# Gate and up products of a feed-forward step in seven block products

## The chip, the core and the metric

The kernel runs on one core of one Trainium2 chip. The metric is the device time of one execution in microseconds. Engines are named as in the profile: PE is TensorE's matmul side and PEld its weight loads, DVE is VectorE, ACT is ScalarE, POOL is GpSimd, SP is SyncE, which here only issues transfers. Each engine works through its own list of instructions in order and waits on semaphores for the others.

## The reference, cut to what matters

Two layers of a decoder trunk run over a prompt of 512 tokens and 8 x 4 sample tokens, 544 tokens in all, with a width of 1024. Four feed-forward half steps of this form stand before and behind the two mixers:

```python
def swiglu(x, w_gu, w_down):
    gate, up = jnp.split(x @ w_gu, 2, axis=-1)
    return (jax.nn.silu(gate) * up) @ w_down

def macaron_half(h, g, w_gu, w_down):
    return h + 0.5 * swiglu(rms_norm(h, g), w_gu, w_down)
```

`w_gu` has 1024 rows and 2 x 2816 columns, `w_down` 2816 rows and 1024 columns, all float32. The order of the stages is f10 (feed-forward 1 of layer 0), the even mixer, f20, f11, the odd mixer, f21.

## The kernel before, in words

Features lie on the partitions, tokens along the free axis: the residual is eight tiles `x` of 128 x 544. Every matrix product of weights (`mm`, L199) is made in three passes: weight and activation are each split into a high part in the float32r format and the rest, a low part (`wh`, `wl` for weights, `h`, `l` for activations), and high x high, high x low and low x high are summed in PSUM. One matmul has 128 x 128 weights and 272 tokens, so each k-tile of a 544-token product takes six matmuls, two halves `a` in the two banks of an `acc` tile. There are two `acc` tiles (two banks each) and four one-bank tiles `ps`.

A feed-forward step (`ffn`) has 22 inner rows `f` of 128 features. `hid(f)` makes one of them: the gate product (eight k-tiles, 48 matmuls), times `rbc`, the 1/rms of each token (L373), Silu on ACT (L374), times `rbc` again (L375), the up product (48 matmuls), the product of both (L378), and the split of the result into `h` and `l` (`split`, L209 on ACT and L210 on DVE). The weights of two inner rows come in one transfer each for gate and up (`stage`, L162, 256 columns, 1 MB) into one of two buffers `S`; `unit` cuts 128 columns out of it, ACT writes `wh` (L184) and DVE `wl` (L185). Each of `wh` and `wl` has two buffers, in a pool `wp` that lives through the whole program.

The inner rows are worked in three parts, (0, 7), (7, 15) and (15, 22). Behind the rows of a part, and one row of the next, its share of the down product is added to the eight `x` tiles (L395). Behind the last part `after_x` splits each finished `x` tile, times the next norm's gain, into the high and low parts (L212, L213) that the next stage multiplies, and adds its squares to `ssum`.

The order of instructions on each engine is set ahead of time by a scheduler that moves ready work forward by priority; weight parts have high priority. The mixers use `mm` too, and between them attention, a state space scan and other work that is not changed here. `mid` is a call in f10 that prepares the attention's position bias; it writes 3 MB from POOL's queue.

## Time and profile before

| what | value |
| --- | --- |
| time, median of 3 runs | 2400.13 us (2396.95 to 2403.28) |
| profiled execution: span | 2398.6 us |
| PE busy | 2367.8 us (99%), 18348 matmuls |
| DVE busy | 1182.6 us (49%) |
| ACT busy | 777.0 us (32%) |
| POOL busy | 163.8 us (7%) |
| read from and written to HBM | 203.69 MB and 17.75 MB |

The profiled execution gives its span from the first to the last instruction; it lies 1.5 us under the median of the runs, and no other time of this execution is shown. In the profile's groups, `acc<-h,wh` is a tile written from tiles read, with the buffer numbers left out. Matmuls overlap, so the mean time of one (about 290 ns) is not the pace at which they follow each other: that is a window's length divided by the count of matmuls in it. In a row of the windows view stand, for each engine, the busy time and the count of instructions, then the clock that was granted to TensorE, the busy share of the transfer engines, and GB/s. In a row of the timeline stand start, duration, engine, line, instruction, and in brackets the idle time before it with what ended it. Rows of one line show the count, the least, the middle and the greatest duration in ns.

### The profile page before, as it was taken

The numbers are of one execution on the slowest core, as the hardware profiler recorded it, in microseconds if no ns is written. First come the engines' busy times: TensorE is split into PE (matmuls) and PEld (weight loads), VectorE is DVE, ScalarE is ACT, GpSimd is POOL, SyncE is SP. The second block draws the span as 40 slices with busy tenths as digits, with TensorE's granted clock in tenths as the row PEclk, the third lists the DMA queues.
The fourth block names the chain that finished last, engine by engine and source line by source line (L and its number), as shares of the span: only waits on it lengthen the run. The fifth ranks groups of instructions, "written<-read, shape, count | busy, mean of one in ns | idle before, by whom it ended". The sixth has DMA issues, their size and how long they took to land.

```text
span 2398.6 us, 41806 instructions
## 1 busy us (share of the span) xinstructions
PE 2367.8 (99%) x18348; PEld 2296.9 (96%) x18348; DVE 1182.6 (49%) x1838; ACT 777.0 (32%) x1201; POOL 163.8 (7%) x199
## 2 busy tenths in 40 slices
...
GB/s 156 84 101 72 136 95 87 114 69 85 119 82 99 145 97 102 84 89 89 88 81 96 86 83 106 71 102 121 77 71 113 79 57 89 82 86 103 74 96 75
DMA packets 216677, 224.14 MB, mean 93 GB/s; under 512 B 8824, under 2 KB 208848, under 8 KB 216496
## 3 DMA queue, kind: packets, MB, share of 16 engines
q1 hardware_dynamic: 210312, 203.84, 26.4%
...
q8 instruction: 145, 2.38, 0.4%
...
HBM read 203.69 MB, written 17.75 MB: 92 GB/s over the span
## 4 chain that ended last, share of the span: by engine, by line
PE 76%; issue 19%; DVE 2%; DMA 2%; ACT 1%; POOL 1%; SPq 0%; POOLq 0%; ACTq 0%; DVEq 0%
PE acc L199 69%; DMA S<-in_ffn_w_down_dram 1%; PE ps L900 1%; PE ps L1129 1%; PE ps L609 1%; PE ps L1173 1%; PE ps L1168 1%; PE ps L601 0%; DMA S<-in_ffn_w_gu_dram 0%; PE ps L269 0%; PE ps L896 0%; PE ps L762 0%; PE ps L1056 0%; PE ps L620 0%; ACT sc L1146 0%
## 5 line engine op out<-in xcount | busy, mean ns | idle before, releaser
L199 PE MATMUL acc<-h,wh 128*128 128x272 f32 x5632 | 1178.6, 290 | 9.7 <-ACT wh L184 8.3
L199 PE MATMUL acc<-l,wh 128*128 128x272 f32 x5632 | 1179.8, 290 | 0.0
L199 PE MATMUL acc<-h,wl 128*128 128x272 f32 x5632 | 1174.4, 289 | 0.0
L199 PEld LDWEIGHTS acc<-h,wh 128*128 128x128 f32 x5632 | 888.5, 189 | 21.0 <-issue 9.1
L199 PEld LDWEIGHTS acc<-l,wh 128*128 128x128 f32 x5632 | 888.2, 189 | 11.1 <-issue 9.7
L199 PEld LDWEIGHTS acc<-h,wl 128*128 128x128 f32 x5632 | 888.4, 189 | 6.1 <-issue 5.2
L184 ACT ACTIVATE wh<-S 128x1024 fp32r<-128x1024 f32 (+1 forms) x361 | 375.2, 1040 | 1375.7 <-PE acc L199 1231.7
L185 DVE TENSOR_TENSOR wl<-S,wh 128x1024 fp32r<-128x1024 f32 (+1 forms) x361 | 436.9, 1210 | 64.9 <-ACT wh L184 54.9
L395 DVE SCALAR_TENSOR_TENSOR x<-acc,x 128x544 f32<-128x544 f32 x96 | 69.5, 724 | 285.4 <-PE acc L199 285.4
L378 DVE TENSOR_TENSOR hf<-acc,t 128x544 f32<-128x544 f32 x88 | 63.8, 725 | 275.6 <-PE acc L199 275.4
L373 DVE TENSOR_TENSOR t<-acc,rbc 128x544 f32<-128x544 f32 x87 | 63.1, 725 | 269.3 <-PE acc L199 269.1
L375 DVE TENSOR_TENSOR t<-t,rbc 128x544 f32<-128x544 f32 x88 | 63.3, 719 | 3.0 <-ACT t L374 3.0
L210 DVE TENSOR_TENSOR l<-hf,h 128x544 fp32r<-128x544 f32 x88 | 63.3, 719 | 2.2 <-ACT h L209 2.2
L209 ACT ACTIVATE h<-hf 128x544 fp32r<-128x544 f32 x88 | 57.3, 651 | 4.4 <-DVE hf L378 4.4
L374 ACT ACTIVATE t<-t 128x544 f32<-128x544 f32 x88 | 57.5, 653 | 2.1 <-DVE t L373 1.9
L256 POOL DMA_DIRECT2D xd<-x x16 | 8.7, 546 | 544.3 <-DVE x L395 544.3
L213 DVE SCALAR_TENSOR_TENSOR l<-x,cols,h 128x544 fp32r<-128x544 f32 x48 | 40.3, 840 | 0.5 <-ACT h L212 0.5
L212 ACT ACTIVATE h<-x,cols 128x544 fp32r<-128x544 f32 x48 | 35.9, 747 | 8.5 <-DVE x L311 8.2
L1066 POOL DMA_DIRECT2D bias<-scr x8 | 5.9, 753 | 446.7 <-PE ps L980 411.7
...
L1146 ACT ACTIVATE sc<-sc,mx 128x256 f32<-128x256 f32 (+1 forms) x64 | 30.0, 471 | 15.9 <-DVE mx L1139 15.9
L416 DVE TENSOR_TENSOR x<-acc,x 128x544 f32<-128x544 f32 x16 | 11.6, 725 | 43.9 <-PE acc L199 43.9
...
## 6 DMA issues: line engine op xcount, KB each, us to landing
...
```

The costliest lines, as they stand in the source:

```text
L184: nc.scalar.activation(hi[:, :nk, :n], src, AF.Copy)
L185: nc.vector.tensor_tensor(lo[:, :nk, :n], src, hi[:, :nk, :n].bitcast(F32), op=ALU.subtract)
L199: self.nc.tensor.matmul(acc[a][:, :HT] if type(acc) is list else acc[:, a, :HT], w[:, k, :], r[:, a * HT:(a + 1) * HT], start=k == order[0 ...
L209: nc.scalar.activation(h, src, AF.Copy)
L210: nc.vector.tensor_tensor(l, src, h.bitcast(F32), op=ALU.subtract)
L212: nc.scalar.activation(h, src, AF.Copy, scale=scale)
L213: nc.vector.scalar_tensor_tensor(l, src, scale, h.bitcast(F32), op0=ALU.mult, op1=ALU.subtract)
L373: nc.vector.tensor_tensor(two(t1), G[:, :, :HT], two(rbc), op=ALU.mult)
L374: nc.scalar.activation(t1, t1, AF.Silu)
L375: nc.vector.tensor_tensor(t1, t1, rbc, op=ALU.mult)
L378: nc.vector.tensor_tensor(two(h), U[:, :, :HT], two(t1), op=ALU.mult)
L395: nc.vector.scalar_tensor_tensor(two(self.x[m]), acc[:, :, :HT], 0.5, two(self.x[m]), op0=ALU.mult, op1=ALU.add)
```

## The change

The gate and up products of one inner row are taken as one 2 x 2 block product and made in seven block products (Winograd's form of Strassen's scheme). The weights' blocks are A11 (gate, even k-tiles), A12 (gate, odd), A21 (up, even), A22 (up, odd); the activations' blocks are B11 and B12 (even k-tiles, first and second 272 tokens), B21 and B22 (odd ones). With S1 = A21 + A22, S2 = S1 - A11, S3 = A11 - A21, S4 = A12 - S2 and T1 = B12 - B11, T2 = B22 - T1, T3 = B22 - B12, N4 = B21 - T2, the products are A11 B11, S2 T2, S3 T3, S1 T1, A12 B21, A22 N4 and S4 B22, each over four k-tiles in the same three passes: 12 matmuls of 272 tokens. An inner row thus has 84 matmuls where it had 96.

- `unit7` loads 128 gate and 128 up columns in two transfers of 512 KB with rows of 512 bytes (one transfer of 1 MB with rows of 1 KB served two inner rows before). POOL adds and subtracts them to S1, S2 (`sa`, L234 and L235 of the changed kernel) and S3, S4 (`sb`, L237 and L238), 128 x 512 each. ACT and DVE (L227, L228) split A11 with A12, S1 with S2 and S3 with S4 (128 x 1024 each) and A22 (128 x 512, `qh` and `ql`). `sa` and `sb` have one buffer each, `wh` and `wl` five, `qh` and `ql` two.
- `mm7` sums the products in four banks, a and d (the two halves of `acc`), b and c (`ps`). ACT copies a after the first product (L266), DVE adds b after the second (L268), c after the third (L270), d after the fourth (L272) and c again after the sixth (L274), 128 x 272 each. The gate is in a for the first 272 tokens and in d plus U for the others, the up part in the tile `u`.
- `hid` multiplies `u` by `rbc` on POOL (L474), the gate by `rbc` on DVE (L475 to L477, 128 x 272 each), takes Silu on ACT (L478), multiplies both (L479) and splits the result (L283 on ACT, L284 on DVE).
- The inner rows are worked in four parts, (0, 6), (6, 12), (12, 17), (17, 22), so the down product is added to `x` in four turns (L496).
- Behind two finished `x` tiles, `pair7` makes and splits the activations' blocks for the next feed-forward step; before a mixer the split is as it was.
- The weight pool `wp` is opened anew for each stage (two buffers in a mixer, five in a feed-forward step). The splits of the attention's result in the odd mixer take other buffers. Comments are gone.

```diff
     POOLS = {"even": MIX(4, 18, 3, 5), "odd": MIX(6, 14, 4, 5)}
-    POOLS.update({k: (("rot", "rot", 6),) for k in ("f10", "f20", "f11", "f21")})
+    POOLS.update({k: (("wp", "wp", 5), ("wq", "wq", 2), ("sp", "sp", 1), ("hl", "hl", 7), ("rot", "rot", 8))
+                  for k in ("f10", "f20", "f11", "f21")})
+    ORDER = (("A11", "B11"), ("S2", "T2"), ("S3", "T3"), ("S1", "T1"), ("A12", "B21"), ("A22", "N4"), ("S4", "B22"))
...
+    def unit7(self, w, f):
+        nc = self.nc
+        s = self.stg.tile([P, 8, 256], F32, name=self.nm("S"), tag="S")
+        for q in range(2):
+            c0 = q * DFF + f * P
+            nc.sync.dma_start(s[:, :, q * P:(q + 1) * P], w[:, c0:c0 + P].rearrange("(k p) m -> p k m", p=P))
+        g0, g1 = s[:, 0::2, 0:P], s[:, 1::2, 0:P]
+        u0, u1 = s[:, 0::2, P:], s[:, 1::2, P:]
+        sa = self.sp.tile([P, 8, P], F32, name=self.nm("sa"), tag="sa")
+        sb = self.sp.tile([P, 8, P], F32, name=self.nm("sb"), tag="sb")
+        G = nc.gpsimd
+        out = {}
+        def parts(src, n, pool, tag, names):
+            hi = pool.tile([P, n, P], F32R, name=self.nm(tag + "h"), tag=tag + "h")
+            lo = pool.tile([P, n, P], F32R, name=self.nm(tag + "l"), tag=tag + "l")
+            nc.scalar.activation(hi, src, AF.Copy)
+            nc.vector.tensor_tensor(lo, src, hi.bitcast(F32), op=ALU.subtract)
+            for nme, sel in names:
+                out[nme] = (hi[:, sel], lo[:, sel])
+        with self.tc.high_priority():
+            parts(s[:, :, 0:P], 8, self.wp, "w", (("A11", slice(0, 8, 2)), ("A12", slice(1, 8, 2))))
+            G.tensor_tensor(sa[:, 0:4], u0, u1, op=ALU.add)
+            G.tensor_tensor(sa[:, 4:8], sa[:, 0:4], g0, op=ALU.subtract)
+            parts(sa, 8, self.wp, "w", (("S1", slice(0, 4)), ("S2", slice(4, 8))))
+            G.tensor_tensor(sb[:, 0:4], g0, u0, op=ALU.subtract)
+            G.tensor_tensor(sb[:, 4:8], g1, sa[:, 4:8], op=ALU.subtract)
+            parts(sb, 8, self.wp, "w", (("S3", slice(0, 4)), ("S4", slice(4, 8))))
+            parts(u1, 4, self.wq, "q", (("A22", slice(0, 4)),))
+        return out
+    def prod(self, acc, w, ops, start, stop):
+        hi, lo = w
+        for j in range(4):
+            rh, rl = ops[j]
+            for q, (a, r) in enumerate(((hi, rh), (hi, rl), (lo, rh))):
+                self.nc.tensor.matmul(acc, a[:, j, :], r, start=start and j == 0 and q == 0,
+                                      stop=stop and j == 3 and q == 2, skip_group_check=True)
+    def mm7(self, w, xs):
+        nc = self.nc
+        V = nc.vector
+        acc, b, c = self.acc(), self.ps(), self.ps()
+        a, b, c, d = acc[:, 0, :HT], b[:, :HT], c[:, :HT], acc[:, 1, :HT]
+        U, r = self.RR("U"), self.RR("u")
+        U2, U3 = U[:, :HT], U[:, HT:]
+        for i, (wn, xn) in enumerate(self.ORDER):
+            to = (a, b, c, d, a, c, d)[i]
+            self.prod(to, w[wn], [xs[j][xn] for j in range(4)], i < 4, i != 0 and i != 2 and i != 3)
+            if i == 0:
+                nc.scalar.activation(U2, a, AF.Copy)
+            elif i == 1:
+                V.tensor_tensor(U2, b, U2, op=ALU.add)
+            elif i == 2:
+                V.tensor_tensor(U3, c, U2, op=ALU.add)
+            elif i == 3:
+                V.tensor_tensor(r[:, HT:], d, U3, op=ALU.add)
+            elif i == 5:
+                V.tensor_tensor(r[:, :HT], c, U2, op=ALU.add)
+        return a, d, U2, r
...
         with self.tc.high_priority():
-            self.xs[k] = self.split(x, self.gain(n, k))
+            if n % 3 == 1:
+                self.xs[k] = self.split(x, self.gain(n, k))
+            elif k % 2:
+                self.pair7(k // 2, n)
...
+    def pair7(self, j, n):
+        A, B, D, E = (self.tmp(s) for s in ("fa", "fb", "fd", "fe"))
...
+        S.activation(A[:, lo_], x0[:, lo_], AF.Copy, scale=g0)
+        S.activation(E[:, lo_], x0[:, hi_], AF.Copy, scale=g0)
+        S.activation(B, x1, AF.Copy, scale=g1)
+        V.tensor_tensor(A[:, hi_], E[:, lo_], A[:, lo_], op=ALU.subtract)
+        V.tensor_tensor(D[:, lo_], B[:, hi_], A[:, hi_], op=ALU.subtract)
+        V.tensor_tensor(D[:, hi_], B[:, hi_], E[:, lo_], op=ALU.subtract)
+        V.tensor_tensor(E[:, hi_], B[:, lo_], D[:, lo_], op=ALU.subtract)
...
+        for src, names in ((A, ("B11", "T1")), (B, ("B21", "B22")), (D, ("T2", "T3"))):
+            h, l = self.split(src)
...
+        S.activation(h, E[:, hi_], AF.Copy)
+        V.tensor_tensor(l, E[:, hi_], h.bitcast(F32), op=ALU.subtract)
...
         def hid(f):
-            if f % 2 == 0:
-                un[0] = self.unit(gu, 0, 8, f * P)
-                un[1] = self.unit(gu, 0, 8, DFF + f * P)
+            a, d, U2, u = self.mm7(self.unit7(gu, f), xs)
             t1 = self.RR("t1")
...
-                G = self.mm(un[0](f % 2), 8, xs)
-                nc.vector.tensor_tensor(two(t1), G[:, :, :HT], two(rbc), op=ALU.mult)
+            r0, r1 = rbc[:, :HT], rbc[:, HT:]
+            nc.gpsimd.tensor_tensor(u, u, rbc, op=ALU.mult)
+            nc.vector.tensor_tensor(t1[:, :HT], a, r0, op=ALU.mult)
+            nc.vector.tensor_tensor(t1[:, HT:], d, U2, op=ALU.add)
+            nc.vector.tensor_tensor(t1[:, HT:], t1[:, HT:], r1, op=ALU.mult)
             nc.scalar.activation(t1, t1, AF.Silu)
-            nc.vector.tensor_tensor(t1, t1, rbc, op=ALU.mult)
-            U = self.mm(un[1](f % 2), 8, xs)
-            h = self.RR("hf")
-            nc.vector.tensor_tensor(two(h), U[:, :, :HT], two(t1), op=ALU.mult)
-            done[f] = self.split(h)
-        parts = [(0, 7), (7, 15), (15, 22)]
+            nc.vector.tensor_tensor(u, u, t1, op=ALU.mult)
+            done[f] = self.split(u, al=self.HL)
+        parts = [(0, 6), (6, 12), (12, 17), (17, 22)]
```

The rows below are lists of instructions as the scheduler left them; their line numbers are those of the kernel that each list is of. The first place is DVE amid the inner rows of a feed-forward step. Before, one inner row has six DVE instructions (weights 1024 wide, everything else 544 wide):

```order
L373 TENSOR_TENSOR t_1117_9212<-acc_9217,rbc_8729 128x544
L185 TENSOR_TENSOR wl_9330<-S_9208,wh_9329 128x1024
L375 TENSOR_TENSOR t_1117_9212<-t_1117_9212,rbc_8729 128x544
L378 TENSOR_TENSOR hf_9322<-acc_9273,t_1117_9212 128x544
L185 TENSOR_TENSOR wl_9386<-S_9210,wh_9385 128x1024
L210 TENSOR_TENSOR l_9325<-hf_9322,h_9324 128x544
```

With the change, DVE has 13 instructions for one inner row. These twelve are followed by `ql_1010`, 128 x 512; `acc_623`, `acc_753` belong to the third and fourth inner row of f10, the weights `wl_864` to `wl_876` to the fifth:

```order
L228 TENSOR_TENSOR wl_864<-S_858,wh_863 128x1024
L475 TENSOR_TENSOR t_145_717<-acc_623,rbc_331 128x272
L476 TENSOR_TENSOR t_145_717<-acc_623,U_626 128x272
L228 TENSOR_TENSOR wl_870<-sa_861,wh_869 128x1024
L268 TENSOR_TENSOR U_756<-ps_754,U_756 128x272
L477 TENSOR_TENSOR t_145_717<-t_145_717,rbc_331 128x272
L270 TENSOR_TENSOR U_756<-ps_755,U_756 128x272
L272 TENSOR_TENSOR u_757<-acc_753,U_756 128x272
L228 TENSOR_TENSOR wl_876<-sb_862,wh_875 128x1024
L479 TENSOR_TENSOR u_627<-u_627,t_145_717 128x544
L284 TENSOR_TENSOR l_725<-u_627,h_724 128x544
L274 TENSOR_TENSOR u_757<-ps_755,U_756 128x272
```

So the weights of an inner row are split about one row ahead, in between the additions of the row that PE works on. On PE the products of neighbouring rows interleave: behind the last product of one row stand the third and fourth product of the next (24 matmuls), then the first product of the row after that, which takes the `acc` tile that L475 and L476 have read.

The second place is POOL at the same time. Before, POOL's list has nothing between the inner rows; now five instructions stand there for each row:

```order
L234 TENSOR_TENSOR sa_861<-S_858 128x512
L235 TENSOR_TENSOR sa_861<-sa_861,S_858 128x512
L237 TENSOR_TENSOR sb_862<-S_858 128x512
L238 TENSOR_TENSOR sb_862<-S_858,sa_861 128x512
L474 TENSOR_TENSOR u_627<-u_627,rbc_331 128x544
```

In a part's list of inner rows, the sets of four (L234 to L238) that stand among the rows rather than in the down product before them number 5, 4, 3 and 2 in the four parts of a step.

The third place is DVE between f20 and f11, right behind the addition (L496) to the last of the eight `x` tiles. `h_13479`, `l_13480` are the split of B11 and T1 of the last pair, `l_13488` that of T2 and T3, the `wl` are the first weights of f11:

```order
L369 TENSOR_TENSOR l_13373<-fe_13364,h_13372 128x272
L228 TENSOR_TENSOR wl_13536<-S_13530,wh_13535 128x1024
L228 TENSOR_TENSOR wl_13542<-sa_13533,wh_13541 128x1024
L228 TENSOR_TENSOR wl_13548<-sb_13534,wh_13547 128x1024
L228 TENSOR_TENSOR wl_13666<-S_13660,wh_13665 128x1024
L284 TENSOR_TENSOR l_13480<-fa_13468,h_13479 128x544
L356 TENSOR_TENSOR fd_13470<-fb_13469,fa_13468 128x272
L357 TENSOR_TENSOR fd_13470<-fb_13469,fe_13471 128x272
L284 TENSOR_TENSOR l_13484<-fb_13469,h_13483 128x544
L339 TENSOR_TENSOR ssum_13111<-ssum_13111,sq_13493 128x544
L358 TENSOR_TENSOR fe_13471<-fb_13469,fd_13470 128x272
L284 TENSOR_TENSOR l_13488<-fd_13470,h_13487 128x544
```

PE's list there has 40 matmuls of f11 (and the norm's two) between the last down product and the first one that reads the T2 and T3 of the last pair. Before, the last `x` tile was only split (one ACT and one DVE instruction), and the first 42 matmuls of f11 did not need it.

35 lines of the change are left out of this document (25 added, 10 removed).

## The prediction

> **What bounds the kernel now.** I read the page first: the share of each engine, the chain that ended last, the costliest groups.
>
> ```profile
> span 2398.6 us, 41806 instructions
> PE 2367.8 (99%) x18348; PEld 2296.9 (96%) x18348; DVE 1182.6 (49%) x1838; ACT 777.0 (32%) x1201; POOL 163.8 (7%) x199
> PE 76%; issue 19%; DVE 2%; DMA 2%; ACT 1%; POOL 1%; SPq 0%; POOLq 0%; ACTq 0%; DVEq 0%
> L184 ACT ACTIVATE wh<-S 128x1024 fp32r<-128x1024 f32 (+1 forms) x361 | 375.2, 1040 | 1375.7 <-PE acc L199 1231.7
> L378 DVE TENSOR_TENSOR hf<-acc,t 128x544 f32<-128x544 f32 x88 | 63.8, 725 | 275.6 <-PE acc L199 275.4
> ```
>
> PE is the bound: it is never idle for long, and ACT and DVE wait for it (the last column), not it for them. The pace comes from the windows view of the middle of f11, and transfers from the waits of the SP queue there:
>
> ```profile
> 1290.00:1660.00 370.00, 370.00 (x2946) 370.00 (x2945) 154.55 (x179) 96.28 (x116) 3.30 (x6) 1.00 0.28 91
> SPq L162 <- DVE wl L185: 361.6, 32, 18.5
> ```
>
> 2946 matmuls in 370 us are 0.1256 us each at full clock, and POOL is nearly idle. SP waits for a free `S` buffer, never the buffer for data: transfers have time to spare.
>
> **What is removed.** 12 matmuls for each of 22 rows in four steps, 1056 x 0.1256 = **-132.6 us**. A row takes PE 84 x 0.1256 = 10.55 us instead of 12.06. I keep the pace: every matmul already has its own weight load. One thing is new, twelve matmuls in a row into one bank, where `mm` changes banks each time. The nearest row is a pair that accumulates into one bank:
>
> ```profile
> 581.61 1.04 PE L900 MATMUL ps<-sT,cm 128*32 128x512 f32 x2
> L900 PE MATMUL ps<-sT,cm x32: 592/592/617, 575.5 to 673.6; 128*32 128x512 f32 x32
> ```
>
> The second starts 1.04 - 0.59 = 0.45 us after the first, before its end, so one bank does not make them wait for each other. The transfers now come in 512-byte pieces, 2048 for 1 MB:
>
> ```profile
> q1 hardware_dynamic: 210312, 203.84, 26.4%
> ```
>
> 26.4% of 16 engines over the span, by 210312 packets, is 0.048 us each. Even at that price for half the bytes, 2048 packets on 16 engines take 6.1 us of the 10.55 us of a row. I price them at nothing; the cover is the spare time above.
>
> **What is added on DVE and POOL.** DVE's durations, alone:
>
> ```profile
> L185 DVE TENSOR_TENSOR wl<-S,wh 128x1024 fp32r<-128x1024 f32 x296 | 366.7, 1239 | 62.0 <-ACT wh L184 54.9
> L185 DVE TENSOR_TENSOR wl<-S,wh 128x896 fp32r<-128x896 f32 x64 | 69.9, 1093 | 2.9
> L1192 DVE TENSOR_TENSOR pc<-acc,rbc 128x272 f32<-128x272 f32 x8 | 3.4, 430 | 0.0
> 1305.21 1.23 DVE L185 TENSOR_TENSOR wl<-S,wh 128x1024 fp32r<-128x1024 f32 x1 [0.17 <-ACT wh L184]
> 1306.35 0.72 DVE L210 TENSOR_TENSOR l<-hf,h 128x544 fp32r<-128x544 f32 x1
> ```
>
> The last two rows start 1.14 us apart though the first lasts 1.23, so back to back an instruction occupies DVE 0.08 us less than its listed time: 1.15 for 1024 elements, 0.64 for 544, 0.35 for 272. 128 elements less save 0.146, so 512 take 1.239 - 0.584 - 0.08 = 0.57. A row's 13 instructions are 3 x 1.15 + 0.57 + 2 x 0.64 + 6 x 0.35 = 7.4 us, under 10.55. ACT has 3.5 x 1.04 and three smaller ones, under 6 us. POOL's 512-wide instructions:
>
> ```profile
> L570 POOL TENSOR_TENSOR sr<-cst_even,da x16: 1028/1042/2063, 520.5 to 675.8; 128x512 f32<-128x512 f32 x16
> L1214 POOL TENSOR_TENSOR ta<-pc x8: 1056/1066/2097, 1762.9 to 1840.5; 128x527 f32<-128x527 f32 x8
> ```
>
> 1.04 for 512, 1.09 for 544 by the slope between the rows: 4 x 1.04 + 1.09 = 5.25 us a row. Each engine alone fits. But the greatest durations are twice the middle ones, and the timeline of the start, where POOL (L262) and DVE work side by side, shows why:
>
> ```profile
> 12.16 1.33 POOL L262 TENSOR_TENSOR ssum<-ssum,sq 128x544 f32<-128x544 f32 x1
> 12.53 1.55 DVE L213 SCALAR_TENSOR_TENSOR l<-x,cols,h 128x544 fp32r<-128x544 f32 x1 [0.25 <-ACT h L212]
> 17.77 0.78 DVE L213 SCALAR_TENSOR_TENSOR l<-x,cols,h 128x544 fp32r<-128x544 f32 x1
> 17.92 1.84 POOL L262 TENSOR_TENSOR ssum<-ssum,sq 128x544 f32<-128x544 f32 x1 [2.65 <-ACT sq L252]
> 20.97 1.68 DVE L185 TENSOR_TENSOR wl<-S,wh 128x1024 fp32r<-128x1024 f32 x1
> 21.64 2.23 POOL L262 TENSOR_TENSOR ssum<-ssum,sq 128x544 f32<-128x544 f32 x1
> 22.57 1.88 DVE L213 SCALAR_TENSOR_TENSOR l<-x,cols,h 128x544 fp32r<-128x544 f32 x1
> 18.56 0.68 DVE L311 COPY x<-ps 128x512 f32<-128x512 f32 x1
> ```
>
> L213 alone takes 0.78. Started while POOL runs (12.16 to 13.49), it ends at 14.08, 0.59 after POOL's end: it did nothing until then. POOL's instruction from 17.92 ends at 19.76, 1.21 after DVE's at 18.55; the one from 21.64 ends 1.22 after DVE's L185. So one waits for the other's end; they do not share. L311, which reads PSUM, passes during POOL's work at its usual 0.68. I take it that DVE instructions with both inputs in SBUF, and POOL's, exclude each other, and that those with an input in PSUM run freely.
>
> The Trainium skill states this rule ("SBUF — State Buffer", section on the two separate sides): the pair of ports that VectorE and GpSimd share is held by one for a whole instruction, and a VectorE instruction with two SBUF inputs needs it against a GpSimd one that reads SBUF. These rows agree (0.78 becomes 1.55).
>
> In a row, such DVE instructions are three `wl`, `ql`, L477, L479 and L284: 3 x 1.15 + 0.57 + 0.35 + 2 x 0.64 = 5.65 us. With POOL's 5.25 that is 10.90 us, **already over PE's 10.55**. The five DVE instructions that read PSUM (1.75 us) come on top where POOL does not run meanwhile: at most 12.65. Between these ends I lay the listed orders side by side, counting from the end of the `wl` of `sa`, which lets POOL start the next row's `sa`. L268 passes under POOL's first instruction, L477 waits for its end at 1.04 and ends at 1.39; POOL's second runs to 2.43 over L270 and L272; `wl` of `sb` ends at 3.58, L479 at 4.22; POOL's third runs to 5.26, L284 to 5.90, POOL's fourth to 6.94 over L274; `ql` ends at 7.51, POOL's L474 at 8.60, `wl` of A at 9.75, L475 and L476 at 10.45, the next `wl` of `sa` at **11.60**. I take 11.6, 1.05 over PE.
>
> PE can use up some lead first: two products (24 x 0.1256 = 3.0 us) stand between a row's last matmul and the one that needs its `acc` back, less 0.7 for L475 and L476 and some 0.3 for the signals, so 2.0 us a part. Only rows whose neighbour's set of POOL work falls in the row stretch count, 5, 4, 3 and 2. A step loses (5.25 - 2) + (4.2 - 2) + (3.15 - 2) + (2.1 - 2) = 6.7 us, four steps **+27 us**; with 10.90 nothing (5 x 0.35 is under 2), with 12.65 21.4 a step, 86 in all. In the down products DVE and POOL have ample room.
>
> **What is added at the seams.** Now PE passes from stage to stage at full pace except before f21, and starts early:
>
> ```profile
> 1935.00:1945.00 10.00, 9.67 (x43) 7.94 (x44) 6.58 (x18) 4.91 (x10) 4.98 (x9) 0.60 0.08 21
> 875.00:885.00 10.00, 10.00 (x82) 10.00 (x81) 6.20 (x10) 4.32 (x5) 0.00 (x0) 1.00 0.58 190
> 1268.00:1278.00 10.00, 10.00 (x79) 9.84 (x78) 5.92 (x9) 3.46 (x4) 0.00 (x0) 1.00 0.21 67
> 1668.00:1678.00 10.00, 10.00 (x79) 9.84 (x78) 5.92 (x10) 3.38 (x4) 0.00 (x0) 1.00 0.39 133
> 10.00:20.00 10.00, 2.85 (x11) 2.60 (x12) 0.73 0.80 271
> 20.00:30.00 10.00, 10.00 (x76) 9.90 (x75) 0.93 0.48 131
> 30.00:40.00 10.00, 9.29 (x71) 8.96 (x71) 1.00 0.64 212
> ```
>
> (the last three count L199 alone). Into f11, the third place in the order: from the last `x` on DVE 0.64 + 0.35 + 4 x 1.15 + 4 x 0.64 + 3 x 0.35 = 9.2 us until `l_13488`; PE has 40 matmuls, 5.0 us: 4.2 lost. Into f20, where two `ql` and the A of the second row come in between, I count 9.35 us for 14 matmuls (1.8), 7.6 lost; into f21 7.9 for the same, 6.1. Into each mixer two weight parts now stand behind the last `x` (0.64 + 2 x 1.15), since `wp` is opened anew: 3 each. At the start DVE is the pace: the pairs cost it 4 x (5 x 0.35 + 3 x 0.64) = 14.7 us where eight splits cost 6.7; three or four weight parts more come before PE's second product (4.0); and eight set instructions of POOL, half of each in DVE's way, 4.2: 16. Together 23.9 + 16 = **+40 us**. Below, 15 (work finds its way forward in the list); above, 60 (an idle PE is granted less clock, 0.73 in the window at 10 us). The stall in f10 behind the 3 MB write of `mid` stays as it is.
>
> **Sum:** 2398.6 - 132.6 + 27 + 40 = 2333.0 us of span, and 1.5 for the median above it: **2334 us**.
>
> **Rivals.**
> The shared port hides (22%): POOL's work slips into DVE's idle time, rows run at PE's 10.55, and the seams cost 30: 2398.6 - 132.6 + 30 + 1.5 = 2298 us. For it: DVE alone needs only 7.4 of 10.55. Against: 10.90 of exclusive work.
> Serial queues (12%): DVE's list is in order, so when a `wl` waits for ACT and that for POOL, the sums for PE's banks behind it wait too. If no PSUM read is covered and each of ten changes of hand costs 0.1, a row takes 13.65, 3.1 over PE: 35.4 a step, 142 in all, 2398.6 - 132.6 + 142 + 40 + 1.5 = 2449 us, slower. The point is a loss of 93 in the rows, 12.8 us a row. Against it: DVE went on 0.59 after POOL's end with no price of its own.
> Weights late (3%): if the 512-byte pieces made a load outlast a row, say 12 us, PE gains nothing: about 2440.
> Not doing what it says (3%): same-bank products at a slower pace; 7392 of them 10 ns slower are 74 us, 2408.
> The rest, 60%, is the forecast.
>
> **How the numbers follow.** A measurement here tells 0.3% (7 us) from no change. All low ends give 2398.6 - 132.6 + 15 + 1.5 = 2282, all high ends 2398.6 - 132.6 + 86 + 60 + 1.5 = 2413. The forecast's own 60% with the hidden case lie mostly in 2286 to 2396: the range is drawn there, and leaves out the serial case, its like, and a little of the forecast's and the hidden case's edges, about 2 in 10. Faster: the hidden case 22 and nearly all of the forecast, 84 with a little of the small rivals; within 0.3%: 6; slower 10.
>
> **What would show it.** The matmul count falls to 17292. In the windows of the row stretches, matmuls per us fall behind 7.96 late in a step's first part and hardly in its last; POOL's L234 to L238 and DVE's L228 have means well over 1.04 and 1.24; PE waits there for DVE (L475, L476, or `wl`). Windows at the seams show some 5 us without work before f20, f11 and f21. It is wrong if POOL's set runs at 1.04 beside DVE (no exclusion), if PE keeps 7.96 in all stretches, or if PE waits for transfers into `S`.

## The result and the profile after

The changed kernel takes 2432.05 us (median of 4 runs, 2424.74 to 2433.87) against 2400.64 us (4 runs, 2396.95 to 2403.28): a ratio of 1.0129, 95% interval 1.0112 to 1.0147. It is slower, by 1.3%. The forecast was 2334 us, and 2396 was the upper end of its range.

The page of the changed kernel, its engines and the chain that ended last:

```profile
span 2429.6 us, 42019 instructions
PE 2281.7 (94%) x17292; PEld 2185.3 (90%) x17292; DVE 1718.3 (71%) x2613; ACT 998.9 (41%) x1578; POOL 866.5 (36%) x639
PE 71%; DVE 15%; issue 5%; DMA 4%; ACT 2%; POOL 1%; SPq 0%; DVEq 0%; POOLq 0%; ACTq 0%
```

The 1056 matmuls are gone, but PE is now idle for 6% of the span, and DVE has risen from 2% to 15% of the chain. To see where, cut the span at the end of the last sum of `x` of each stage (the eighth L496 of a step's last part, the sixteenth L517 of a mixer; L395 and L416 before). A feed-forward step should have lost 132.6 / 4 = 33.2 us:

| stage | before | after | difference | lost against the pure matmul gain |
| --- | --- | --- | --- | --- |
| f10 | 430.5 | 454.5 | +24.0 | 57.2 |
| even mixer | 437.1 | 443.8 | +6.7 | 6.7 |
| f20 | 399.5 | 394.9 | -4.6 | 28.6 |
| f11 | 399.9 | 391.5 | -8.4 | 24.8 |
| odd mixer | 322.3 | 341.1 | +18.8 | 18.8 |
| f21 | 402.8 | 397.3 | -5.5 | 27.7 |

The last column says how much of the expected gain is missing: 164 us in all, where the prediction had 67. The loss inside the rows can be taken from the distances of one row's L476 to the next where no down product stands between. In f20 they are 12.6, 12.7, 12.2, 12.7, 8.4 and 11.7 us in the first part (70.3 against 6 x 10.55 = 63.3), 55.6 against 52.75 in the second, 42.8 against 42.2 in the third: 7.0 + 2.85 + 0.6 = 10.4 us, and nearly the same in each step; the fourth part loses nothing (31.4 against 31.65). The stretch with the first down products behind `mid` takes 68.1 us in f10 and 46.5 in f20, 21.6 more; before, the second part of f10 took 155.8 against 145.0, 10.8 more: f10's middle lost another 10.8. What is left of a stage is put down to its seam, the passage from one stage to the next; it is a remainder and holds what is lost at the stage's end too:

| term | predicted | measured |
| --- | --- | --- |
| rows, four steps | 27 | 42 |
| start of f10 | 16 | 36.0 |
| into f20, f11, f21 | 7.6, 4.2, 6.1 | 18.2, 14.4, 17.3 |
| even and odd mixer | 3, 3 | 6.7, 18.8 |
| middle of f10 (behind `mid`) | 0 | 10.8 |

The start of f10, where the kernel before had 71 to 77 matmuls in 10 us from 20 us on, in the windows view of the changed kernel (all engines):

```profile
20.00:40.00 20.00, 6.38 (x23) 5.06 (x23) 20.00 (x21) 9.40 (x14) 14.54 (x10) 0.50 0.18 52
40.00:60.00 20.00, 7.86 (x31) 6.40 (x31) 18.01 (x27) 10.03 (x17) 9.26 (x6) 0.53 0.18 54
```

54 matmuls in 40 us. DVE is listed as busy for 38 of them and POOL for 24, the time in which one waits for the other included, and the granted clock is about half.

A row stretch, in the timeline of the changed kernel (POOL's and DVE's rows of one stretch, put in one fence each):

```profile
941.37 1.28 POOL L234 TENSOR_TENSOR sa<-S 128x512 f32<-128x512 f32 x1 [2.51 <-issue]
942.73 1.37 POOL L235 TENSOR_TENSOR sa<-sa,S 128x512 f32<-128x512 f32 x1
945.26 1.28 POOL L237 TENSOR_TENSOR sb<-S 128x512 f32<-128x512 f32 x1 [1.17 <-DVE wl L228]
```

```profile
941.15 0.43 DVE L268 TENSOR_TENSOR U<-ps,U 128x272 f32<-128x272 f32 x1
941.51 1.44 DVE L477 TENSOR_TENSOR t<-t,rbc 128x272 f32<-128x272 f32 x1
943.22 1.96 DVE L228 TENSOR_TENSOR wl<-sb,wh 128x1024 fp32r<-128x1024 f32 x1
945.45 1.67 DVE L479 TENSOR_TENSOR u<-u,t 128x544 f32<-128x544 f32 x1
```

The forecast exclusion can be read off these rows: L268, which reads PSUM, passes at 0.43 beside POOL; L477, 0.43 alone, takes 1.44 and ends 0.30 us after L234; the next `wl` ends 1.08 after L235. The order is not quite that of the hand timeline, where L479 stands ahead of POOL's third operation: here L237 goes first, and L479 ends 0.58 after it. What is not as forecast is POOL's price, from the view of one line:

```profile
L234 POOL TENSOR_TENSOR sa<-S x88: 1266/1290/6882, 15.2 to 2359.7; 128x512 f32<-128x512 f32 x88
L238 POOL TENSOR_TENSOR sb<-S,sa x88: 1267/1776/2292, 23.7 to 2366.3; 128x512 f32<-128x512 f32 x88
L474 POOL TENSOR_TENSOR u<-u,rbc x88: 1342/1811/2352, 68.4 to 2386.0; 128x544 f32<-128x544 f32 x88
```

Not one of them runs at 1.04: even the fastest 512-wide one takes 1.27, the fastest 544-wide one 1.34.

### The profile page after: what moved, and what is told of

Read it like the earlier page. It is cut to its first block, busy times and chain, and to the rows that moved or that the text cites. A ratio compares the mean times of both kernels' runs of the same rounds, so it can differ in the third digit from the quotient of the medians.

```text
span 2429.6 us, 42019 instructions
## 1 busy us (share of the span) xinstructions
PE 2281.7 (94%) x17292; PEld 2185.3 (90%) x17292; DVE 1718.3 (71%) x2613; ACT 998.9 (41%) x1578; POOL 866.5 (36%) x639
## 3 DMA queue, kind: packets, MB, share of 16 engines
q1 hardware_dynamic: 302088, 203.85, 27.7%
## 4 chain that ended last, share of the span: by engine, by line
PE 71%; DVE 15%; issue 5%; DMA 4%; ACT 2%; POOL 1%; SPq 0%; DVEq 0%; POOLq 0%; ACTq 0%
PE acc L205 37%; PE acc L249 15%; PE ps L249 12%; DVE wl L228 5%; DMA S<-in_ffn_w_gu_dram 3%; DVE ql L228 2%; DVE wl L191 1%; DVE l L284 1%; DVE u L479 1%; ACT h L283 1%; PE ps L1001 1%; DVE t L476 1%; DVE t L475 1%; DVE x L496 1%; PE ps L1231 1%
## 5 line engine op out<-in xcount | busy, mean ns | idle before, releaser
L205 PE MATMUL acc<-l,wh 128*128 128x272 f32 x2832 | 600.2, 292 | 0.0
L205 PEld LDWEIGHTS acc<-h,wh 128*128 128x128 f32 x2832 | 450.7, 191 | 41.0 <-issue 16.7
L205 PEld LDWEIGHTS acc<-l,wh 128*128 128x128 f32 x2832 | 450.9, 190 | 10.2 <-issue 8.8
L205 PEld LDWEIGHTS acc<-h,wl 128*128 128x128 f32 x2832 | 450.8, 190 | 7.1 <-issue 5.3
L249 PE MATMUL acc<-h,wh 128*128 128x272 f32 x1408 | 413.3, 294 | 46.4 <-DVE x L496 18.8
L249 PE MATMUL acc<-l,wh 128*128 128x272 f32 x1408 | 411.0, 292 | 9.7 <-DVE l L284 9.7
L190 ACT ACTIVATE wh<-S 128x1024 fp32r<-128x1024 f32 (+2 forms) x217 | 193.6, 897 | 347.5 <-PE acc L205 197.9
L234 POOL TENSOR_TENSOR sa<-S 128x512 f32<-128x512 f32 x88 | 123.9, 1408 | 587.9 <-DMA S<-in_ffn_w_gu_dram 185.0
L249 PEld LDWEIGHTS acc<-h,wh 128*128 128x128 f32 x1408 | 269.0, 191 | 53.3 <-issue 19.0
L249 PEld LDWEIGHTS acc<-h,wl 128*128 128x128 f32 x1408 | 269.8, 192 | 20.0 <-DVE wl L228 20.0
L249 PEld LDWEIGHTS acc<-l,wh 128*128 128x128 f32 x1408 | 269.6, 191 | 11.6 <-DVE l L284 11.6
L191 DVE TENSOR_TENSOR wl<-S,wh 128x1024 fp32r<-128x1024 f32 (+2 forms) x217 | 231.5, 1068 | 58.1 <-ACT wh L190 54.4
L474 POOL TENSOR_TENSOR u<-u,rbc 128x544 f32<-128x544 f32 x88 | 162.2, 1844 | 235.6 <-DVE u L274 235.6
L249 PE MATMUL ps<-h,wh 128*128 128x272 f32 x704 | 206.3, 293 | 9.3 <-ACT wh L227 5.8
L249 PE MATMUL ps<-h,wl 128*128 128x272 f32 x704 | 204.6, 291 | 0.9
L249 PE MATMUL ps<-l,wh 128*128 128x272 f32 x704 | 204.3, 290 | 0.0
L237 POOL TENSOR_TENSOR sb<-S 128x512 f32<-128x512 f32 x88 | 136.1, 1546 | 145.3 <-DVE wl L228 143.5
L228 DVE TENSOR_TENSOR wl<-S,wh 128x1024 fp32r<-128x1024 f32 x88 | 165.5, 1881 | 22.1 <-ACT wh L227 20.5
L228 DVE TENSOR_TENSOR ql<-S,qh 128x512 fp32r<-128x512 f32 x88 | 107.7, 1225 | 84.3 <-ACT qh L227 82.9
```

Source lines behind the costliest of these rows:

```text
L190: nc.scalar.activation(hi[:, :nk, :n], src, AF.Copy)
L191: nc.vector.tensor_tensor(lo[:, :nk, :n], src, hi[:, :nk, :n].bitcast(F32), op=ALU.subtract)
L205: self.nc.tensor.matmul(acc[a][:, :HT] if type(acc) is list else acc[:, a, :HT], w[:, k, :], r[:, a * HT:(a + 1) * HT], start=k == order[0 ...
L228: nc.vector.tensor_tensor(lo, src, hi.bitcast(F32), op=ALU.subtract)
L234: G.tensor_tensor(sa[:, 0:4], u0, u1, op=ALU.add)
L237: G.tensor_tensor(sb[:, 0:4], g0, u0, op=ALU.subtract)
```

## The experiments

Line numbers are those of the changed kernel; in an experiment they can be shifted by a few lines. A run's stages are cut as in the table above. Stages that an edit should not touch still differ by up to 5 us between runs (the odd mixer takes 345.7 us in mid_split, which changes only f10, and 341.1 in the changed kernel), so that only larger differences are read. Each median is of the number of runs given.

### Is it the port? no_pool, unread, sums_dve

```diff
# no_pool
-            G.tensor_tensor(sa[:, 0:4], u0, u1, op=ALU.add)      (and the three others, and L474)
-            parts(sa, 8, ...);  parts(sb, 8, ...)
+            parts(s[:, :, P:], 8, ...);  parts(s[:, :, 0:P], 8, ...)
# unread: as no_pool, but the five GpSimd operations stay, L474 into a tile of its own
# sums_dve
-        G = nc.gpsimd
+        G = nc.vector
-            nc.gpsimd.tensor_tensor(u, u, rbc, op=ALU.mult)
+            nc.vector.tensor_tensor(u, u, rbc, op=ALU.mult)
```

> Left out: GpSimd's five operations of an inner row (L234, L235, L237, L238, L474). The seven products are given halves of plainly split weights, and the up value is not multiplied by the norm; everything else stays. Port theory (VectorE and GpSimd exclude each other, VectorE 7.4 us and GpSimd 5.8 us of a row add up): rows fall from 12.6 to the 10.55 us of 168 matmuls, the 42 us lost inside the rows go, the starts of the feed-forward steps lose less too, time 2330 to 2370. Pace theory (TensorE runs the rows' 272-column matmuls more slowly by itself): rows stay above 12, time above 2410. Late-sum theory (no exclusion; TensorE only waits because a sum of weights comes late from GpSimd's queue): the same as the port theory here; the next run tells these two apart.

> Left out: only the readers of GpSimd's results. GpSimd does its five operations of a row as before, on the same operands, but nothing waits for them: the products take plainly split weights and the up value as it is. Port theory: VectorE is still shut out for 5.8 us a row, rows of 12 to 12.7 us in the first two parts, time 2400 to 2440. Late-sum theory: nobody waits for a sum, rows of 10.6 us, time 2330 to 2370.

> GpSimd's five operations of a row are given to VectorE, nothing is left out. Port theory: VectorE has 7.4 + 4 x 0.57 + 0.64 = 10.3 us of work a row and nobody to exclude it, just under TensorE's 10.55: rows of 10.6 to 10.9 us, about 35 us less in the rows and some less at the starts, time 2370 to 2395. Help theory (GpSimd takes work off an engine that is already short of time): rows of 12.6 us or more, time 2430 to 2470.

Measured: no_pool 2369.53 us, unread 2446.33 (one run each), sums_dve 2402.29 (10 runs), ratio to the kernel before 1.0017 (1.0007 to 1.0028). In the windows view, 50 us of f20's first rows, the changed kernel, then no_pool, unread and sums_dve:

```profile
928.00:978.00 50.00, 46.08 (x347) 43.82 (x346) 46.89 (x53) 22.75 (x30) 31.61 (x20) 1.00 0.26 79
```

```profile
905.00:955.00 50.00, 48.58 (x384) 48.15 (x383) 36.05 (x57) 24.90 (x33) 0.00 (x0) 1.00 0.32 96
```

```profile
938.00:988.00 50.00, 47.37 (x357) 45.21 (x356) 46.82 (x55) 22.42 (x30) 35.28 (x19) 1.00 0.27 80
```

```profile
920.00:970.00 50.00, 45.68 (x356) 44.80 (x355) 45.52 (x75) 23.10 (x32) 0.00 (x0) 1.00 0.27 83
```

Read the first count in brackets, PE's: 347, 384, 357 and 356 matmuls (at 0.1256 us each, 50 us hold 398). In unread nobody waits for GpSimd, and the rows stay as slow (taken by L477, the first six distances are 68.5 us in f20's start of unread and 68.9 in the changed kernel). So it is not a sum that comes late; GpSimd's mere work on SBUF slows VectorE.

With all five operations on VectorE it does 75 instructions in nearly the same busy time as 53 before, and the kernel gains 30 us. Little of that is in the rows: the long ones get shorter (11.9 us in place of 12.2 to 12.7) and the short ones longer (10.3 in place of 8.4), and the 21 distances of a step add up to 332.9 us in f20 where they were 333.2, 6 us less over the four steps. The rest is gained at the seams and in the mixers: f10 takes 448.8 us, f20 389.9, f21 390.6.

Several of the numbers expected were off: sums_dve is slower than its 2370 to 2395 and unread than its 2400 to 2440, and the long rows fall to 11.9 us, not 10.6 to 10.9, since DVE's 18 instructions of a row occupy it for 3 x 1.15 + 5 x 0.60 + 3 x 0.64 + 7 x 0.35 = 10.8 us (the 512-wide ones list 0.68, 0.60 back to back) and its waits for ACT come on top. Without any GpSimd work (no_pool) the six distances are still 65.9 us, not 63.3; what these 2.6 us are was not taken apart.

### What takes the seams: no_pair7, no_both

```diff
# no_pair7 (no_both: this and no_pool)
-        A, B, D, E = ...            (three ACT scalings, four DVE sums, four splits a pair)
+        for src, g, names in ((x0, g0, ...), (x1, g1, ...)):
+            h, l = self.split(src, g)
```

> Left out: the four sums of halves of each pair of residual tiles and their splits (helper pair7, L341 to L372); each tile is split once, as in the kernel before, and the halves are given to the seven products. Operand theory (the chain of sums on VectorE and ScalarE is what keeps TensorE empty at the start of a feed-forward step): 15 us less at the start of the first step, 5 us at each of the three others, time about 2400. Weight theory (TensorE waits there for the prepared weights, whatever the operands): less than 8 us in all, time 2422 or more.

> Left out: both what no_pool and what no_pair7 leave out (GpSimd's five operations of a row; the sums of halves of the pairs and their splits). The first row ends 32.5, 31.6 and 33.3 us after the last x in f20, f11 and f21 and at 73.5 us in f10; in the kernel before it was 16.6 three times and 40.8. Load theory (the seams are the time that VectorE and GpSimd take, one behind the other, for the last pairs' sums and the first rows' weights): without both, first rows end after 20 to 23 us, and at 50 to 54 us in f10; no_pool's and no_pair7's gains at the seams add up. Order theory (TensorE may take only 9 matmuls of the first product ahead of the last pair, and weights of later rows stand in front): the two gains overlap, 24 to 27 us and 56 to 62 us, as with either alone.

Measured: no_pair7 2396.52 us, no_both 2344.64 (one run each). The time from the last `x` to the end of the first row's L477:

| | f10 (from 0) | f20 | f11 | f21 |
| --- | --- | --- | --- | --- |
| after | 73.5 | 32.5 | 31.6 | 33.3 |
| no_pool | 63.7 | 27.2 | 26.1 | 24.3 |
| no_pair7 | 61.6 | 27.9 | 29.0 | 24.8 |
| no_both | 50.4 | 26.0 | 22.0 | 23.5 |

In f10 the gains are 9.8 and 11.9, together 23.1; in f11 5.5 and 2.6, together 9.6: there they add up, and what is gained was load on VectorE and GpSimd. It is not all of the loss: no_both's span is 2342.9 us, where 2398.6 - 132.6 would be 2266.0, so that 77 of the 164 us are lost without any of these sums (f10 28.9, f20 13.5, f11 9.2, f21 11.2, the mixers 3.4 and 11.0). The start of f10 in no_both:

```profile
20.00:40.00 20.00, 11.22 (x52) 9.37 (x52) 14.80 (x22) 9.01 (x15) 11.09 (x5) 0.65 0.18 53
40.00:60.00 20.00, 20.00 (x162) 20.00 (x161) 15.00 (x24) 10.69 (x13) 0.00 (x0) 1.00 0.36 106
```

In f20 and f21 the gains overlap (5.3 and 4.6 give 6.5; 9.0 and 8.5 give 9.8). What is left and what is gained can be told apart in time. The first 10 us behind the mixer's last `x` and the stretch from there to the first row's L476, in f20 of the changed kernel, then of no_both:

```profile
898.30:908.30 10.00, 3.43 (x14) 2.35 (x14) 9.88 (x13) 7.25 (x12) 4.87 (x3) 0.67 0.37 106
908.30:927.00 18.70, 16.09 (x110) 15.41 (x111) 13.23 (x17) 6.02 (x8) 14.79 (x9) 0.90 0.19 57
```

```profile
866.60:876.60 10.00, 5.52 (x27) 4.37 (x28) 8.47 (x11) 6.20 (x9) 0.00 (x0) 0.85 0.23 66
876.60:890.30 13.70, 13.70 (x96) 13.49 (x95) 8.01 (x13) 4.77 (x7) 0.00 (x0) 0.86 0.32 96
```

A stretch less its matmuls at 0.1256 us each is what TensorE lost there:

| lost, us | f20 | f11 | f21 |
| --- | --- | --- | --- |
| first 10 us, changed kernel | 8.2 | 5.5 | 8.5 |
| from there to the first row, changed kernel | 4.9 | 6.1 | 5.8 |
| first 10 us, no_both | 6.6 | 4.7 | 6.0 |
| from there to the first row, no_both | 1.6 | 0 | 0 |

So the load is what is lost behind the first 10 us. GpSimd is shut out there as well: its first L234 behind the last `x` takes 4.60 us in f20 and 6.88 in f11, ACT waits for that `sa`, and VectorE then stands idle for 3.6 and 4.8 us, waiting for ACT's `wh`. The first 10 us lose nearly as much without the sums. What stands there shows in the timeline of no_both, DVE from the mixer's last `x` on:

```profile
865.92 0.72 DVE L496 TENSOR_TENSOR x<-acc,x 128x544 f32<-128x544 f32 x1 [3.12 <-PE acc L205]
866.81 5.77 DVE L226 TENSOR_TENSOR wl<-S,wh 128x1024 fp32r<-128x1024 f32 x5 [0.17 <-ACT wh L225]
872.50 1.28 DVE L226 TENSOR_TENSOR ql<-S,qh 128x512 fp32r<-128x512 f32 x2
873.70 0.78 DVE L281 SCALAR_TENSOR_TENSOR l<-x,cols,h 128x544 fp32r<-128x544 f32 x1
```

Five weight parts and two of A22, nearly two rows' worth, stand between the last `x` and the split of the last tile that the first row's products need.

### Why so late there: early_w, early_w2, early_w3

The weight tiles of a step lie on memory of the stage before. Three layouts of the pools (groups of buffers) were tried:

```diff
# early_w (also: hi and lo of a part in one tile): the mixers' small tiles, uu, rot, ld first, then wp, aux; steps: sp, wp, wq, ...;
#          f20 and f11 share one set of pools
# early_w2: wp one pool of 2 for the program; unit7's parts in a pool w7 of 4; rot 8 -> 6
# early_w3: wp of 5 kept; a pad in f20's and f21's pools puts tiles 0, 3 and 4 on ld, uu, sm, rot
```

> Nothing is left out, GpSimd keeps its five operations. Pools alone are moved: the first three weight parts and the sums of a feed-forward step lie on memory that the mixer before it has left early (its small tiles, uu, rot and ld) and no longer on its weight tiles; f20 and f11 share one set of pools, so that the rotation of weight tiles goes on from one to the other. Memory theory (at a seam the first row's weights are prepared only behind the last matmul of the stage before, together with the last pair's sums): ACT's first L227 of a step stands some us ahead of the last x in place of behind it, and f20, f11 and f21 lose 6 to 10 us less each, time 2402 to 2414. Chain theory (the pairs' sums and VectorE's total work set the seam anyway): less than 3 us each, time 2422 or more.

> Nothing is left out, GpSimd keeps its five operations. In early_w the second and third part of the first row still got memory of the mixer's weight tiles. Here wp is one pool for the whole program, as in the kernel before, and the row's parts have four tiles of their own (w7) that lie on the mixer's small tiles, ld and uu, all left early; rot of the feed-forward steps has 6 tiles in place of 8. Memory theory: ACT's first L227 operations of a step end before the last x, f20, f11 and f21 lose 6 to 10 us less each, the odd stage falls to 326 to 330 as its small tiles lie on memory that is left before the last part's down products, time 2390 to 2404. Chain theory: the three steps change by less than 3 us each; only the odd stage gains, time 2414 to 2422.

> Nothing is left out, GpSimd keeps its five operations. As early_w2, but without its price: the five weight tiles stay together and rot keeps 8 tiles; the pools of each step are laid out so that the three tiles that a step takes first lie on ld, uu, sm and rot of the mixer before it. Memory theory: the first rows of f20 and f21 end 6 and 12 us sooner after the mixer's last x, as in early_w2 (26.7 and 20.8 us against 32.5 and 33.3), and now these steps keep it: f20 at 386 to 391, f21 at 384 to 390, f11 within 3 us of 391.5, time 2408 to 2420. Chain theory: f20 and f21 within 3 us of 394.9 and 397.2.

Measured, one run each: 2423.64, 2472.64, 2433.07 us. early_w missed its aim at f20 and f21: in f20 the second part (`sa`) still waited for the mixer's last matmul. Into f11 the first row came 6 us sooner (25.4 us in place of 31.6), but f20 before it took 404.1 us in place of 394.9, so that the two together gained nothing. early_w2 brought the first rows forward (26.7, 27.8 and 20.8 us in place of 32.5, 31.6 and 33.3), but with fewer weight tiles the 21 distances of a step grew by 16 us. early_w3 gives the early memory alone: f20 and f21 take 398.3 and 397.6 us, as before. Early memory alone does not help these two. The trace of early_w3 shows why, DVE in f20 from the mixer's last `x` (two more low parts, of `sa` and `sb`, stand between the first two `w` rows):

```profile
898.85 0.72 DVE L518 TENSOR_TENSOR x<-acc,x 128x544 f32<-128x544 f32 x1 [2.22 <-PE acc L207]
899.49 1.22 DVE L229 TENSOR_TENSOR w<-S,w 128x1024 fp32r<-128x1024 f32 x1
902.89 2.29 DVE L229 TENSOR_TENSOR w<-S,w 128x1024 fp32r<-128x1024 f32 x1
905.10 3.44 DVE L229 TENSOR_TENSOR ql<-S,qh 128x512 fp32r<-128x512 f32 x2
908.46 1.50 DVE L357 TENSOR_TENSOR fd<-fb,fa 128x272 f32<-128x272 f32 x1
```

ACT has made the high parts of the first row by the end of the mixer, but in DVE's list their low parts, the second row's and both `ql` still stand behind that `x` and ahead of the last pair's sums (L357), and POOL's sums of the second row stretch them (3.44 for two `ql` that take 1.28 in no_both). DVE was idle for 2.22 us ahead of `x`, while the first of this work, its high part written at 897.1, stood behind `x` in its list.

Weights first in the list are no cure either. In f21 of early_w2 the three low parts of the first row and both `ql` stand ahead of the last `x` (L517) on DVE; below are the two `ql`, that `x`, and PE's longest wait there:

```profile
2061.86 1.28 DVE L228 TENSOR_TENSOR ql<-S,qh 128x512 fp32r<-128x512 f32 x2
2063.06 0.71 DVE L517 TENSOR_TENSOR x<-acc,x 128x544 f32<-128x544 f32 x1
PE acc L249 <- DVE x L517: 7.3, 1, 7.3
```

The first 10 us behind the last `x`, changed kernel and early_w2:

```profile
2025.80:2035.80 10.00, 3.26 (x12) 2.30 (x12) 10.00 (x10) 7.50 (x11) 5.77 (x5) 0.61 0.36 105
```

```profile
2063.80:2073.80 10.00, 8.90 (x52) 8.45 (x53) 7.62 (x15) 5.59 (x9) 0.00 (x0) 0.79 0.70 208
```

52 matmuls stand there in place of 12, but that `x` itself is late and PE loses 7.3 us ahead of it. From 20 us ahead of the last `x` to the first row, 11.4 us are lost in place of 16.5.

### The odd mixer: early_odd

```diff
-        qk = sm("qk", [P, 2])  ...  sink, sk8, gq, loaded on entering the mixer
+        gq, gk, sink, sk8 = self.odd_small      # loaded in mid, in f10
         ...
-        ext = ...      # pool rows: load, eight transposes (L1081)
+        ...            # the same, behind the keys and values
```

> Nothing is left out. The odd mixer's small loads (qk, sink, sk8) and the product that makes gq are done in the middle of the first step, and the block that loads and transposes the carried pool rows (ext) stands behind the keys and values. Small-load theory (the odd mixer starts late because VectorE's L1058 and TensorE's L1081 stand ahead of the first products in their lists and wait for loads that cannot start before f11's memory is free): the stage from f11's last x to the odd mixer's last x falls from 341 us to 326 to 330, all others stay, time 2416 to 2422. Weight theory (w_in's first tile is late by itself): less than 4 us, time 2428 or more.

Measured: 2419.51 us (one run), the odd stage 328.9 in place of 341.1. The waits of DVE and of PE at the start of this stage, changed kernel:

```profile
DVE gq L1058 <- DMA qk<-in_d_q_norm_dram: 12.4, 1, 12.4
```

```profile
PE acc L205 <- DVE kv L1095: 6.3, 1, 6.3
PE ps L1081 <- DMA pst<-in_state_pool_dram: 4.7, 2, 4.5
```

Of these only 0.5 us (PE on `kv`) is left in early_odd. The windows of the first 20 us behind f11, changed kernel and early_odd:

```profile
1685.00:1705.00 20.00, 15.09 (x101) 13.74 (x102) 4.52 (x5) 5.02 (x6) 9.33 (x16) 0.89 0.75 224
```

```profile
1685.00:1705.00 20.00, 19.29 (x147) 18.71 (x148) 10.24 (x14) 5.96 (x8) 9.27 (x16) 1.00 0.73 228
```

So two in-order lists stopped for small loads that start behind f11; in the kernel before DVE has no wait for them there. Why they start so late can be seen from early_w, whose odd stage took 326.7 us with the loads left where they were and only the pools moved: in the changed kernel their memory belongs to f11's pools until its end. This accounts for 12 to 14 of the 19 us.

### The middle of f10: mid_split, wq1

```diff
# mid_split
-        nc.gpsimd.dma_start(rows, self.bc(pat, 1, P))            # 3 MB at once
+        ... eight pieces, one issued in each of the next eight hid(f)
# wq1
-    ... ("wq", "wq", 2) ...
+    ... ("wq", "wq", 1) ...
```

> Nothing is left out, GpSimd keeps its five operations. The 3 MB write of the position bias (scr, in the middle of f10) goes out in eight pieces, one with each of the next eight rows, in place of one. Transfer theory (the 10.7 us that f10 loses beyond the other steps in its second part are S waiting for a DMA system that this write fills, with loads in 512-byte pieces): the stretch from row 11 to row 12 of f10 falls from 68.1 us to 48 to 56, f10 by 12 to 20 us, the other stages stay, time 2411 to 2420. If another part of the middle is late (the columns, the transposes, the order of the lists), f10 changes by less than 4 us.

> Nothing is left out, GpSimd keeps its five operations. wq has one buffer in place of two, so that the part ql of the next row cannot be made before the sixth product of this row; in VectorE's list it falls behind the last sums of x of a part (in f10's middle) and, at the seams, behind the last pair's sums. List theory (VectorE's list is in order, and a weight part of a later row that waits, for its transfer or for GpSimd, stands ahead of work that TensorE waits for): TensorE's wait for L496 in f10's middle falls from 18.8 us to 7 to 10 (a wl of the same late tile still stands ahead of the very last x), f10 by 8 to 11 us; the first rows of f20 and f21 end 2 to 4 us sooner; time 2410 to 2421. If the wait is the transfer's alone, f10 changes by less than 3 us; if the one buffer starves the sixth product, rows get longer than 12.7 us and the time is over 2432.

Measured: 2437.30 and 2423.36 us (one run each). mid_split decided nothing: the scheduler moved all eight issues together, and the load of the next row's `S` took as long as with one (view of the line, then the chain of waits):

```profile
L483 POOL DMA_DIRECT2D scr<-pat x8: 566/566/590, 254.4 to 258.3; - x8
255.88 33.41 DMA S<-in_ffn_w_gu_dram
```

mid_split's f10 takes 460.6 us, 6 more. The changed kernel's chain has the same load with 35.80 us, and the kernel before one of 28.46. What differs besides is what the load stops. PE's waits from 215 to 310 us, before, after, and in wq1:

```profile
PE acc L199 <- ACT wh L184: 7.7, 1, 7.7
```

```profile
PE acc L249 <- DVE x L496: 18.8, 1, 18.8
```

```profile
PE acc L249 <- ACT U L266: 10.4, 1, 10.4
PE ps L249 <- ACT wh L227: 3.4, 1, 3.4
```

After the change PE waits not for weights but for `x` (L496): the `ql` of a later row, whose `S` is late, stands ahead of the last two L496 in DVE's list, and until these have read their `acc` PE has no bank. With one `wq` buffer `ql` falls behind them, PE's wait is 13.8 us, the stretch from row 11 to row 12 falls from 68.1 us to 60.5, and f10 takes 449.0 in place of 454.5: about half of the 10.8 us. At the seams into f20 and f21 wq1 gains nothing (398.6 and 397.3 us). In f20 one `ql` does move behind the last pair's sums, but two of these sums then run beside GpSimd and take 1.50 us each in place of 0.43, and the split of T2 and T3 ends 8.5 us behind the last `x` as against 8.3: there the order alone, with GpSimd at work, brought nothing.

### Rows among the down products: spread, and the versions built on it

```diff
# spread (pool hl 7 -> 11 tiles, rot 8 -> 6)
-        parts = [(0, 6), (6, 12), (12, 17), (17, 22)]
+        parts = [(0, 4), (4, 8), (8, 12), (12, 16), (16, 22)]
...
             for mp in range(4):
                 ... two down products
+                if f1 < 22 and mp < 3:
+                    rows(f1 + 2 + mp)          # one row of the next part
# all1 = sums_dve + early_odd + early_w, the first row's four first products taken pair by pair,
#        the first ssum on VectorE;  all2: pools of early_w2;  all3: all1 with its pools as in
#        the changed kernel, + spread;  all4 = all3 + mid_split;  all5 = all4 + early_w3;
#        all6 = all5 + wq1
```

> Nothing is left out, GpSimd keeps its five operations. Rows and down products are mixed: five parts of 4, 4, 4, 4 and 6 rows, and behind each pair of down products of a part stands one row of the next part (hl has 11 tiles in place of 7, rot 6 in place of 8). Port theory: a row needs 12.6 us of VectorE and GpSimd together and 10.55 of TensorE, a pair of down products 6.0 us of TensorE and about 3 of VectorE; mixed, 15.6 stand against 16.6, so TensorE is the bound again except in the first four and the last two rows of a step. Of the 10.4 us that rows lose in a step 4 to 6 are left, 16 to 25 us less in all, time 2405 to 2416. If rows lose time for another reason (their own order, banks, transfers), mixing does not help: 2425 to 2440.

> Nothing is left out. The five operations on VectorE, the odd mixer's small loads early, the pools moved as in early_w, the first step's sum of squares on VectorE, and in each step's first row the first four products taken pair by pair, so that TensorE has 36 matmuls ahead of the last pair in place of 9. If the losses found one by one add up: 2402 (the operations on VectorE) - 13 (odd mixer) - 25 (three seams) - 12 (first rows) - 5 (start) = 2347, range 2335 to 2375, faster than the kernel before. If the seams are set by VectorE's total work, with the rows at 11.9 us: 2380 to 2400, no gain that can be measured over the kernel before.

> Nothing is left out. As all1 (the five operations on VectorE, small loads early, the first step's sum of squares on VectorE, the first four products of a first row pair by pair), with the pools of early_w2. Memory theory: the seams lose 8 us less each than in all1, time 2370 to 2385. Chain theory: 2395 to 2405.

> Nothing is left out. As all1 but with the pools of the changed kernel, and with rows and down products mixed as in spread. VectorE alone has 10.8 us a row and 3 a pair of down products, 13.8 against TensorE's 16.6: rows at TensorE's pace but for the first ones of a step, 12 to 15 us less a step than in all1. Time 2335 to 2360, faster than the kernel before. If VectorE's rows are bound by the order of its list and not by its load, no gain over all1: 2395 to 2410.

> Nothing is left out. all3 with the bias written in eight pieces. If the middle's loss is the transfer's and does not depend on GpSimd: f10 12 to 20 us less than in all3, time 2353 to 2361. If not: 2370 to 2375.

> Nothing is left out. all4 with the pools of early_w3 (hl of f21 has 10 tiles in place of 11). Memory theory: f20 and f21 lose 5 to 10 us less each than in all4, time 12 to 18 us under all4's. If VectorE's total work sets the seams once GpSimd is out of its way: within 4 us of all4.

> Nothing is left out. all5 with one buffer for wq. List theory: 6 to 14 us less than all5, 2352 to 2360. If the rows pay for the missing buffer: 2366 or more.

| | us (runs) | ratio to before, 95% interval |
| --- | --- | --- |
| spread | 2447.28 (1) | |
| all1 | 2403.83 (10) | 1.0018 (1.0009 to 1.0028) |
| all2 | 2418.18 (1) | |
| all3 | 2372.81 (4) | 0.9890 (0.9873 to 0.9906) |
| all4 | 2371.68 (4) | 0.9882 (0.9866 to 0.9899) |
| all5 | 2366.05 (4) | 0.9863 (0.9848 to 0.9878) |
| all6 | 2367.38 (4) | 0.9866 (0.9849 to 0.9882) |

all1 gains nothing over sums_dve (2402.29) and lies near the second of its expectations (2380 to 2400): the odd mixer takes 330.2 us in place of 335.4, but f20 395.6 and f21 395.1 in place of 389.9 and 390.6. all2, with the fewer weight tiles of early_w2, is slower than both of its expectations, spread slower than both of its own, and all3 lies between its two. The pair that tells most is spread and all3. all3 differs from it by more than GpSimd, but in the middle of a step only by that, so that 120 us of f20's middle compare the same mixing with and without GpSimd:

```profile
1110.00:1230.00 120.00, 115.26 (x908) 113.73 (x907) 99.46 (x117) 45.81 (x63) 53.27 (x35) 1.00 0.31 93
```

```profile
1110.00:1230.00 120.00, 120.00 (x959) 120.00 (x958) 99.73 (x160) 48.71 (x65) 0.00 (x0) 1.00 0.33 96
```

959 matmuls in 120 us are 0.1251 us each: TensorE's full pace, with the seven products. Mixing failed in spread though the loads would have fitted, and the timeline of spread shows how:

```profile
1121.54 1.62 POOL L238 TENSOR_TENSOR sb<-S,sa 128x512 f32<-128x512 f32 x1
...
1121.93 1.82 DVE L479 TENSOR_TENSOR u<-u,t 128x544 f32<-128x544 f32 x1
...
1123.78 0.66 ACT L283 ACTIVATE h<-u 128x544 fp32r<-128x544 f32 x1 [2.79 <-DVE u L479]
1124.35 0.38 ACT L266 ACTIVATE U<-acc 128x272 f32<-128x272 f32 x1
```

L479 (0.72 alone) waits for POOL, ACT's L283 waits for L479, and L266, which copies the first product out of its bank, stands behind L283 in ACT's list; PE waits 0.7 us for it in each row (4.7 us in the seven rows of this window). A delay of the port reaches TensorE through two in-order lists, on engines that are not full. all4 and all6 do not differ from all3 and all5 by more than these runs can tell. all5 is the fastest version found, 1.4% under the kernel before; all6 cannot be told from it.

## Why the prediction was wrong, step by step

- **Removed, -132.6 us: right.** 17292 matmuls as counted, and all3 shows their pace unchanged (0.1251), so the same bank twelve times in a row costs nothing. Transfers in 512-byte pieces cost nothing in the rows either; PE waits for none there.
- **Exclusion of DVE and POOL: right, and the rival in which it hides is refuted** (unread). The Trainium skill's rule ("SBUF — State Buffer", the two separate sides), that the shared ports are held for a whole instruction, agrees with these runs (0.43 becomes 1.44). The size was off: 42 us, not 27, and that it was not further off is luck, since two errors offset each other. The first is "1.04 for 512". The quoted row L570 has broadcast inputs and L1214 adds a tile to itself, shifted by a few elements; the sums added here take at least 1.27, and L474 1.34 in place of 1.09. The nearest row was in the prediction itself, L262 with 1.33 for 544. 4 x (1.27 - 1.04) + 0.25 = 1.17 on the hand timeline's 11.60 gives 12.8, and the long rows measure 12.2 to 12.7. The second is the count of long rows, 5, 4, 3 and 2 a step with 2.0 us of lead: with 12.8 us each it would give over 90 us. Measured are four long distances in the first part and one in the second; the second part begins with two of 11.4 and 11.5 us in which PE does 91 and 92 matmuls, its full pace. The weights prepared during the down products carry it further than the prediction allowed.
- **A slip in the sum of a row.** "A row's 13 instructions" adds up 12: seven, not six, are 272 wide, and six of these read PSUM. DVE alone has 7.75 us, not 7.4, and the upper end is 13.0, not 12.65 (105 us in the rows, not 86). The hand timeline has all 13, so that the forecast does not hang on it.
- **Seams, +40: this step failed most.** Measured are 85.9 us at the four steps, against 33.9 for these four. What was priced into f20, f11 and f21 was the time until DVE has split the last pair, and that price was nearly right: 7.6, 4.2 and 6.1 forecast, 8.2, 5.5 and 8.5 lost in the first 10 us. What was put at nothing is all that comes behind it: 4.9, 6.1 and 5.8 us up to the first row, where GpSimd and VectorE shut each other out, and some 11 us that the table's terms hold at the ends of these steps, not taken apart. In f10, 36.0 us against 16, the sums of GpSimd and those of the pairs lie one behind the other; leaving out both brings the first row 23.1 us forward. What the first 10 us lose without any of these sums (6.6, 4.7 and 6.0) stays open: the first row's weights stand there, but early memory (early_w3) changes nothing, and weights ahead of the last `x` (early_w2, f21) make that `x` late.
- **Mixers, +3 each: 6.7 and 18.8, wrong above all for the odd one.** The step looked at `wp` alone. That other pools of a stage open on its predecessor's memory too, so that small loads are late, and that an unimportant L1058 stops a list, was not priced. early_odd showed 12 us of it, early_w 14; the rest was not taken apart.
- **"The stall in f10 stays as it is": wrong, 11 us.** The list now has `ql` ahead of L496, and wq1 showed half of it. The load that `ql` waits for takes 35.8 us where the one before took 28.5; whether that is the other half no run shows.
- **The upper end.** The bound of 60 for the seams took in the clock but not these. With the measured terms the prediction's own sum gives 2398.6 - 132.6 + 42 + 122 + 1.5 = 2431.5, against the measured 2432, as it must, since the terms were taken from the stages of this span.
- **The rival of serial queues** named the time's side and one of the mechanisms (in-order lists), but for the rows, at 13.65 us each; the long ones took 12.2 to 12.7. It was the lists at the seams and in the middle that cost.
